# A transformer block on eight cores: pacing weight casts, keeping x on chip, contiguous attention tiles, and re-ordered weight loads

## The chip, the cores and the metric

The kernel runs on the 8 cores of one Trainium2 chip (two dies, cores 0 to 3 and 4 to 7). The batch has four sequences of 4096 tokens. Each core owns half a sequence (2048 tokens), reads the keys of the other half itself, and never talks to another core. The metric is the device time of the slowest core in microseconds (us). Fast executions of one kernel agree closely (eight of the kernel before, in the rounds of e9_all: 4768.13 to 4791.93 us, 0.5% apart). Some executions fall into a slower state, in which the cores of one die, or of both, show a lower TensorE clock (0.814 to 0.818 on one die in a run of the changed kernel, 5048.91 us; 0.895 to 0.903 on both in one of e9_all, 4639.74 us; against 0.976 to 0.986 in the fast runs of these two); those runs are marked slow and are not compared with fast ones.

Five engines matter: PE (TensorE, matmul), ACT (ScalarE, exponentials and casts), DVE (VectorE), POOL (GpSimd) and SP (SyncE, which here only issues transfers). The GpSimd queue also issues the transfers that convert float32 to bfloat16 on the way ("casts").

## The reference, cut to what matters

```python
D_MODEL, BATCH, SEQ = 2048, 4, 4096          # FFN_HIDDEN = 5632, head width 128
def _hybrid_layer(x, w_in, ...):
    qa, ka, va, qb, kb, vb, ga, gb = split(x @ w_in)
    # A: 8 query heads, 2 key/value heads, full attention over 4096 keys
    out_a = _gqa_blocks(rope(rms(qa)) * scale, rope(rms(ka)), va)          # (B, S, 1024)
    # B: 12 heads in 3 groups with dilation 1, 4, 16; 129 keys per query;
    #    the three groups are combined weighted by their softmax denominators
    out_b = _dilated_window_attention(qb * scale, kb, vb)                  # (B, S, 512)
    mixed = (sigmoid(ga + b0) * (out_a @ w_proj_a)
             + sigmoid(gb + b1) * (out_b @ w_proj_b)) @ w_out
    x = layer_norm(ALPHA * x + mixed)
    h = silu(x @ w_ffn_gate) * (x @ w_ffn_up)
    return layer_norm(ALPHA * x + h @ w_ffn_down)
```

## The kernel before

A small scheduler records every operation, derives the semaphores from which tiles it reads and writes, and emits each engine's instructions in program order. Each engine works through its own list in that order; the timelines below show it for VectorE, which stands idle 1.22 us ahead of a sum whose input is not ready. The stages follow one another:

1. QKV of A for the core's own tokens and keys of all 4096.
2. Attention A: 32 blocks (8 heads by 4 token blocks) of 16 steps. Between the steps, PE is fed "filler" matmuls: B's K, V and Q projections. Their results are copied out of PSUM by VectorE and stored to memory. In the same stage the GpSimd queue casts the later weights to bfloat16 in memory.
3. Attention B, with some of the gate projections as filler.
4. Merge, output projection with the first norm, feed-forward, and a tail.

Cuts are marked with three dots:

```python
# the casts of later weights: 1 MB written by each, issued in attention A's loop
for kc in range(0, 16, 2):
    pre.append((wo_s[kc:kc + 2], wo_d[kc:kc + 2], [("wo", kc), ("wo", kc + 1)]))
for j in range(22):
    pre.append((wfg_s[j], wfg_d[j], [("wg", j)]))
    pre.append((wfu_s[j], wfu_d[j], [("wu", j)]))
...
# filler: one 512-column result is copied to one of three small buffers and stored
def stage_out(bk, n, dst_list, key):
    g = SG[sg_n[0] % 3]
    sg_n[0] += 1
    s.copy("dve", g[:, 0:n], bk[:, 0:n])
    for dst, src in dst_list(g):
        s.dma("sp", dst, src, wk=[key])
...
# attention A, one step
s.actf(pt[:, :], sp_t[:, :], AF.Exp, scale=SCALE)
...
fil.run_to(min(1.0, (G + 1) / NPC))
...
precast_to(int((G + 1) * 88 / NPC))
```

```python
# attention B: a "quad" is four 128-query tiles. Tiles of dilation 4 and 16 are read with that stride.
for j in range(4):
    quads.append((hh, 0, [(0, 4 * j + a) for a in range(4)], j))
    quads.append((hh, 1, [(a, j) for a in range(4)], j))
...
    s.mm(st[...], BK[g][:, kk:kk + dil * 127 + 1:dil], BQ[g][:, q0:q0 + dil * 127 + 1:dil])
    s.stt(st3[...], st3[...], SCALE, bb[...], ALU.mult, ALU.add)          # bias, VectorE
    s.actf(pb[:, :], st[:, :], AF.Exp)                                    # ScalarE
    s.tt("dve", DS[t % 3][...], pb4[:, :, 0, :], pb4[:, :, 1, :], ALU.add)  # sum of key pairs
    ...  # two quads later: probabilities times V into num, sums into den;
    ...  # dilation 4 is accumulated in PSUM on top of dilation 1
    o = num[:, a * 128:(a + 1) * 128] if g != 1 else num[:, r:512:4]
    ...
    elif g == 1:
        s.tt("dve", ACD[:, cs], den, ACD[:, cs], ALU.add)
        s.tt("dve", ACN[:, cs], num, ACN[:, cs], ALU.add)
        s.actf(ACD[:, cs], ACD[:, cs], AF.Ln)
        s.actf(ACD[:, cs], ACD[:, cs], AF.Exp, scale=-1.0)
        s.tt("dve", OB[hh][:, cs], ACN[:, cs], ACD[:, cs], ALU.mult)
```

```python
# output projection: norm and cast of a token tile follow its matmuls
p6_ln(tt)        # statistics and centring on VectorE, scale and shift on GpSimd
p6_cast(tt)      # ScalarE: bfloat16 copy for the transposes
...
# feed-forward: ScalarE's SiLU after each column group
s.actf(sg[:, :], pg, AF.Silu)
```

The softmax here doesn't subtract the row's maximum and nothing guards it: scores larger than these inputs give would overflow.

## Time and profile before

The three runs that set the baseline gave 4788.51, 4779.18 and 4795.51 us. The profiled execution's slowest core is core 4, 4789.8 us long. The stages below are cut at events: the first exponential of attention A, the first of attention B, the first matmul of the merge, of the output projection and of the feed-forward, and the last matmul. Spans are medians over the eight cores, in us.

| stage | span before |
|---|---|
| QKV of A | 272.8 |
| attention A with B's projections | 1480.1 |
| attention B | 211.7 |
| merge | 608.4 |
| output projection | 288.3 |
| feed-forward | 1857.6 |
| tail | 51.7 |

The page of the kernel before: busy time per engine, then the span in 40 slices with PE's busy share, PE's granted clock and the DMA engines' busy share in tenths.

```profile
PE 4141.3 (86%) x19504; PEld 1906.2 (40%) x19504; DVE 1244.5 (26%) x1842; ACT 1005.3 (21%) x1221; POOL 485.4 (10%) x374
...
PE   7953867666998888989889979999999999999995
...
PEclk9976989888999989999999999999999999999997
DMA  8676376386345347331223556555545554554533
```

PE is the engine that bounds it, and its largest holes are in slices 3 to 15. The table by stretches of the kernel before, cut at core 4's stages (start and end, length, then busy us of PE, weight loads, DVE, ACT and POOL with counts, the mean granted PE clock, the DMA share and GB/s), for attention A, attention B, merge and feed-forward:

```profile
274.30:1765.60 1491.30, 1079.42 (x4826) 475.57 (x4827) 475.68 (x723) 560.31 (x577) 71.78 (x138) 0.87 0.55 83
1765.60:1983.50 217.90, 192.96 (x1189) 113.19 (x1188) 119.09 (x160) 94.94 (x118) 6.72 (x13) 0.93 0.68 168
1983.50:2589.60 606.10, 548.63 (x2433) 242.37 (x2432) 132.41 (x193) 89.95 (x131) 29.22 (x55) 0.95 0.23 44
...
2879.50:4738.10 1858.60, 1838.50 (x8480) 829.58 (x8480) 220.37 (x327) 142.93 (x217) 108.25 (x24) 0.99 0.51 170
```

Attention A lasts 1491 us for 1079 us of PE work; the feed-forward has no room. PE's waits before (waiting engine and line, what released it, us in total, times, the longest):

```profile
PE pbig L156 <- DVE SG_111 L192: 128.4, 16, 32.1
PE pbig L156 <- DVE SG_112 L192: 114.2, 15, 44.1
PE pbig L156 <- DVE SG_113 L192: 93.1, 18, 21.5
...
PE pbig L156 <- DMA WG_186<-wfg_s: 32.0, 1, 32.0
PE pbig L156 <- DMA WGT_160<-wgb: 23.6, 4, 8.3
```

336 us are waits for VectorE to copy a filler result into one of the three SG buffers. VectorE is not slow: one copy takes 0.68 us. It waits for the buffer, whose store has not landed (the largest of these waits; us in total, times, the longest):

```profile
DVE SG_111 L192 <- DMA vb_s<-SG_111: 89.3, 3, 35.9
```

At the same time the casts on the GpSimd queue take this long from issue to landing (count, KB, median us):

```profile
wfg_s<-wfg POOLq DMA_DIRECT2D x22, 1024.0 KB, 44.2
...
wo_s<-wo POOLq DMA_DIRECT2D x8, 1024.0 KB, 55.8
```

In attention B the strided tiles cost PE time. The score matmuls of dilation 16 and of dilation 4 before (duration in ns: shortest, median, longest):

```profile
L156 PE MATMUL pbig<-BQ_121,BK_124 x128: 398/422/428, 1762.0 to 1943.0; 128*128 128x128 bf16 x128
...
L156 PE MATMUL pbig<-BQ_123,BK_126 x128: 275/297/314, 1783.9 to 1973.2; 128*128 128x128 bf16 x128
```

The same tile of dilation 1 takes 219 ns. Last, a view that the prediction looked at too little: VectorE's timeline over one pair of quads (dilation 1 and 4) in attention B before. Columns: start us, duration us, engine, line, operation, output and inputs, and in brackets how long the engine sat idle just before and what ended it.

```profile
1920.58 0.43 DVE L176 TENSOR_TENSOR DS_136<-PB_133 128x512 bf16<-128x512 bf16 x1 [1.22 <-ACT PB_133 L170]
1920.93 0.68 DVE L176 TENSOR_TENSOR ACD_120<-pbig,ACD_120 128x512 f32<-128x512 f32 x1
1921.53 0.68 DVE L176 TENSOR_TENSOR ACN_119<-pbig,ACN_119 128x512 f32<-128x512 f32 x1
1923.23 0.69 DVE L176 TENSOR_TENSOR OB_117<-ACN_119,ACD_120 128x512 bf16<-128x512 f32 x1 [1.02 <-ACT ACD_120 L170]
1923.84 1.23 DVE L188 SCALAR_TENSOR_TENSOR pbig<-pbig,BB_130 128x1024 f32<-128x1024 f32 x1
1926.29 0.43 DVE L176 TENSOR_TENSOR DS_137<-PB_134 128x512 bf16<-128x512 bf16 x1 [1.22 <-ACT PB_134 L170]
1926.63 1.23 DVE L188 SCALAR_TENSOR_TENSOR pbig<-pbig,BB_131 128x1024 f32<-128x1024 f32 x1
1929.07 0.43 DVE L176 TENSOR_TENSOR DS_138<-PB_135 128x512 bf16<-128x512 bf16 x1 [1.22 <-ACT PB_135 L170]
```

A pair takes 1929.07 - 1920.58 = 8.5 us. VectorE adds a bias, then stands 1.22 us until ScalarE's exponential of that same quad is done, because the sum DS is next in its list. It stands another 1.02 us for ScalarE's logarithm and exponential, because the product OB is next. Three such pauses, 3.5 us, belong to every pair although VectorE is busy only 119 us of the stage's 218.

### The profile page before, as it was taken

How to read it: one execution, taken by the hardware profiler on the slowest of the kernel's cores; microseconds unless marked ns; L12 is line 12 of the kernel's file. 1: busy time of each engine (PE TensorE's matmuls, PEld its weight loads, DVE VectorE, ACT ScalarE, POOL GpSimd, SP SyncE). 2: the span in 40 equal slices, each digit the busy share in tenths (PEclk: the TensorE clock that was granted, in tenths of full speed). 3: DMA queues.
4: the chain of work that ended last, by engine and by line, in shares of the span. 5: the costliest groups of instructions: out<-in, count | busy, mean ns of one | idle time of the engine just before them, and what ended most of it. 6: DMA issues, size and time to landing. Idle time of an engine off the chain costs nothing.

```text
span 4789.8 us, 50993 instructions; the slowest of 8 cores (4749.5 to 4789.8 us)
## 1 busy us (share of the span) xinstructions
PE 4141.3 (86%) x19504; PEld 1906.2 (40%) x19504; DVE 1244.5 (26%) x1842; ACT 1005.3 (21%) x1221; POOL 485.4 (10%) x374
## 2 busy tenths in 40 slices
PE   7953867666998888989889979999999999999995
PEld 4521323223343334534334434444444444444442
DVE  3531323322343335421112541100110111011102
ACT  1221434333454434311110211000110011001100
POOL 3320000000000000000000560000100011001103
PEclk9976989888999989999999999999999999999997
DMA  8676376386345347331223556555545554554533
GB/s 133 135 112 85 55 97 85 53 113 92 74 91 86 55 109 183 96 76 25 37 36 111 167 171 226 166 160 163 191 167 167 172 185 166 164 172 173 183 123 110
DMA packets 194974, 594.35 MB, mean 124 GB/s; under 512 B 53808, under 2 KB 102768, under 8 KB 162672
## 3 DMA queue, kind: packets, MB, share of 16 engines
q1 hardware_dynamic: 167504, 444.21, 28.5%
q0 software_dynamic: 27232, 146.88, 21.8%
q8 instruction: 160, 2.62, 0.2%
q14 instruction: 78, 0.64, 0.0%
HBM read 668.03 MB, written 147.46 MB: 170 GB/s over the span
## 4 chain that ended last, share of the span: by engine, by line
PE 73%; DMA 12%; another core or an unknown queue 5%; DVE 3%; issue 2%; POOL 2%; ACT 2%; SPq 1%; POOLq 0%; DVEq 0%; ACTq 0%
PE pbig L156 72%; DMA kb_s<-SG_112 2%; DMA vb_s<-SG_113 2%; SPq L146 1%; DMA qb_s<-SG_113 1%; DMA kb_s<-SG_113 1%; DMA XF_73<-xT 1%; DMA WV_76<-wva 1%; DMA WGT_160<-wgb 1%; DMA WGT_162<-wgb 1%; POOL YY_177 L176 1%; PE pbig L154 1%; DMA kb_s<-SG_111 1%; DMA WR_101<-wvb 1%
## 5 line engine op out<-in xcount | busy, mean ns | idle before, releaser
L170 ACT ACTIVATE SGL_205<-pbig 128x512 f32<-128x512 f32 x88 | 52.6, 598 | 947.3 <-PE pbig L156 947.2
L156 PE MATMUL pbig<-WD_193,HT_192 128*128 128x512 bf16 x944 | 224.4, 384 | 10.0 <-DMA WD_193<-wfd_s 9.3
L156 PE MATMUL pbig<-WD_194,HT_192 128*128 128x512 bf16 x944 | 220.6, 381 | 4.6 <-DMA WD_194<-wfd_s 4.3
L156 PE MATMUL pbig<-WD_195,HT_192 128*128 128x512 bf16 x928 | 218.4, 383 | 5.5 <-DMA WD_195<-wfd_s 5.2
L176 DVE TENSOR_TENSOR HT_192<-SGL_206,pbig 128x512 bf16<-128x512 f32 x88 | 60.5, 688 | 536.2 <-PE pbig L156 536.2
L176 DVE TENSOR_TENSOR HT_192<-SGL_205,pbig 128x512 bf16<-128x512 f32 x88 | 60.6, 688 | 503.5 <-PE pbig L156 499.1
L170 ACT ACTIVATE PT_106<-pbig 128x1024 bf16<-128x1024 f32 x128 | 131.1, 1025 | 236.2 <-PE pbig L156 197.7
L170 ACT ACTIVATE PT_105<-pbig 128x1024 bf16<-128x1024 f32 x128 | 131.1, 1024 | 203.2 <-PE pbig L156 152.3
L170 ACT ACTIVATE PT_107<-pbig 128x1024 bf16<-128x1024 f32 x128 | 131.2, 1025 | 176.6 <-PE pbig L156 128.0
L188 DVE SCALAR_TENSOR_TENSOR YY_154_196<-XR_158_200,pbig 128x512 f32<-128x512 f32 x16 | 11.0, 688 | 585.7 <-PE pbig L156 585.7
L176 POOL TENSOR_TENSOR YY_154_196<-YY_154_196,LNP_162_204 128x2048 f32<-128x2048 f32 x8 | 36.9, 4608 | 1231.4 <-DVE YY_154_196 L183 1230.8
L170 ACT ACTIVATE SGL_206<-pbig 128x512 f32<-128x512 f32 x88 | 52.6, 597 | 510.3 <-PE pbig L156 510.3
L170 ACT ACTIVATE PT_108<-pbig 128x1024 bf16<-128x1024 f32 x128 | 130.6, 1020 | 98.4 <-PE pbig L156 77.7
L156 PEld LDWEIGHTS pbig<-WD_193,HT_192 128*128 128x128 bf16 x944 | 92.7, 99 | 125.9 <-issue 18.6
L156 PEld LDWEIGHTS pbig<-WD_194,HT_192 128*128 128x128 bf16 x944 | 92.3, 98 | 117.9 <-issue 8.7
L156 PE MATMUL pbig<-X1T_184,WG_186 128*128 128x512 bf16 x480 | 111.4, 386 | 32.0 <-DMA WG_186<-wfg_s 32.0
L156 PEld LDWEIGHTS pbig<-WD_195,HT_192 128*128 128x128 bf16 x928 | 91.1, 99 | 118.4 <-issue 11.9
L170 ACT ACT_TABLE_LOAD x29 | 37.2, 1283 | 352.8 <-DVE MV_52 L994 249.2
L156 PE MATMUL pbig<-X1T_184,WU_191 128*128 128x512 bf16 x480 | 108.5, 379 | 0.0
L156 PE MATMUL pbig<-X1T_184,WU_189 128*128 128x512 bf16 x480 | 108.5, 379 | 0.0
L156 PE MATMUL pbig<-X1T_185,WU_190 128*128 128x512 bf16 x480 | 108.5, 379 | 0.0
L156 PE MATMUL pbig<-X1T_185,WG_187 128*128 128x512 bf16 x480 | 108.5, 379 | 0.0
(766 smaller groups left out, 7284.8 us busy)
## 6 DMA issues: line engine op xcount, KB each, us to landing
WG_186<-wfg_s SPq DMA_DIRECT2D x30, 1024.0 KB
WU_189<-wfu_s SPq DMA_DIRECT2D x30, 1024.0 KB
WD_193<-wfd_s SPq DMA_DIRECT2D x59, 512.0 KB
WD_194<-wfd_s SPq DMA_DIRECT2D x59, 512.0 KB
WG_187<-wfg_s SPq DMA_DIRECT2D x29, 1024.0 KB
WU_190<-wfu_s SPq DMA_DIRECT2D x29, 1024.0 KB
WG_188<-wfg_s SPq DMA_DIRECT2D x29, 1024.0 KB
WU_191<-wfu_s SPq DMA_DIRECT2D x29, 1024.0 KB
```

The lines of the kernel that those rows point to most:

```text
L146: return self.add(q, lambda e: e.dma_start(out=out, in_=in_), ins, outs, rk, wk, dma=True)
L154: fn = lambda e: e.matmul(out, lhsT=lhsT, rhs=rhs, start=start, stop=stop, skip_group_check=True)
L156: fn = lambda e: e.matmul(out, lhsT=lhsT, rhs=rhs, start=start, stop=stop)
L170: return self.add("act", lambda e: e.activation(out=out, in_=in_, func=func, **kw), ins, [out])
L176: return self.add(eng, lambda e: e.tensor_tensor(out=out, in0=a, in1=b, op=op), [a, b], [out])
L188: return self.add("dve", lambda e: e.scalar_tensor_tensor(out=out, in0=a, scalar=sc, in1=b, op0=op0, op1=op1), ins, [out])
```

## The change

Its intent, part by part:

- **Casts:** half-size (0.5 MB written), each waiting for an exponential of attention A so that they come evenly; 32 of the down-projection's casts move to the merge.
- **x kept on chip:** two buffers of 16 KB per partition hold the far x; their last contents are what B's halo needs, so it is not loaded again. B's K and Q are staged per head in one buffer KS and stored once per head.
- **B's tiles:** K and Q are stored residue by residue, so every tile is contiguous. Dilation 4 is then no longer in token order with dilation 1, so it gets its own evacuation with strided adds.
- **Merge:** gate A of all four token blocks, then gate B, so each weight tile is done sooner. All of B's first loads are issued ahead.
- **Output projection and feed-forward:** weights prefetched; the transposes of the last tiles moved.
- **Tail:** the last half of the last down projection runs tile by tile from 22 resident weight tiles, so only the last tile's norm follows the last matmul.

The diff, cut to its core (cuts marked):

```diff
     for j in range(22):
-        pre.append((wfg_s[j], wfg_d[j], [("wg", j)]))
-        pre.append((wfu_s[j], wfu_d[j], [("wu", j)]))
+        for q in range(2):
+            c = slice(q * 2048, (q + 1) * 2048)
+            pre.append((wfg_s[j][:, c], wfg_d[j][:, c], [("wg", j, q)]))
+            pre.append((wfu_s[j][:, c], wfu_d[j][:, c], [("wu", j, q)]))
...
-            s.dma("pool", o, i, wk=k)
+            s.dma("pool", o, i, wk=k, after=after)
...
-        self.n_dma = {"sp": 16, "pool": 8}
+        self.n_dma = {"sp": 24, "pool": 16}
...
+    far = [(6, 0), (7, 1), (4, 0), (5, 1)]          # last two stay in XH for B's halo
+    for i, (tb, b) in enumerate(far):
+        pair_mms(WK, XH[b], tb, 1, k_dst(tb))
...
+                        if dil == 1:
+                            s.copy("dve", KS[:, tb * 512:tb * 512 + n], bk[:, 0:n])
+                        else:
+                            i0 = tb * 512 // dil
+                            s.copy("dve", KS[:, 0:tot].rearrange("p (r i) -> p r i", r=dil)[:, :, i0:i0 + n // dil],
+                                   bk[:, 0:n].rearrange("p (i r) -> p r i", r=dil))
+                        if tb == nt_list[-1][0]:
+                            s.dma("sp", dst[:, 0:tot], KS[:, 0:tot], wk=[key])
...
-            s.actf(pt[:, :], sp_t[:, :], AF.Exp, scale=SCALE)
+            ex = s.actf(pt[:, :], sp_t[:, :], AF.Exp, scale=SCALE)
+            precast_to(NPRE * (G + 1) // NPC, ex)
```

```diff
         for j in range(4):
+            quads.append((hh, 1, [(a, j) for a in range(4)], j))
             quads.append((hh, 0, [(0, 4 * j + a) for a in range(4)], j))
-            quads.append((hh, 1, [(a, j) for a in range(4)], j))
...
-                    s.mm(st[...], BK[g][:, kk:kk + dil * 127 + 1:dil], qap)
+                    s.mm(st[...], k_tile(g, r, k0), q_tile(g, r, n))
...
             elif g == 1:
+                def view(t_):
+                    return t_[:, cs].rearrange("p (i r) -> p r i", r=4)
+                s.tt("dve", view(ACN), num.rearrange("p (a c) -> p a c", c=128), view(ACN), ALU.add)
+                s.tt("dve", view(ACD), den.rearrange("p (a c) -> p a c", c=128), view(ACD), ALU.add)
+            else:
                 s.tt("dve", ACD[:, cs], den, ACD[:, cs], ALU.add)
                 s.tt("dve", ACN[:, cs], num, ACN[:, cs], ALU.add)
...
+    p6_ln(14)
+    p6_cast(14)
+    p6_ln(15)
+    p6_cast(15)
...
-    late_tr = [14, 15]
+    late_tr = [13, 14, 15]
...
+    WDF = [at("WDF", ...) for i in range(22)]       # resident weights of the last half
...
+    for tl in range(4):                             # last half, one token tile at a time
+        for fb in range(2):
+            for hp in range(22):
+                ... s.mm(b, HT[...], WDF[hp][...], hc == 0, hc == NHC - 1)
+            evac(tl, 1, fb, b)
```

## The prediction

> **What bounds it now.** TensorE: the page gives 86% busy, the other engines at most 26%. In fully busy stretches a 128x512 matmul issues every 215 to 217 ns (table by stretches: 465 per 100 us, clock 1.00), so only PE's holes can shrink. [...] here all eight hold 0.99 through the feed-forward[...]. By stage (span us, PE busy):
> - QKV of A: 0-275, 242
> - attention A with B's projections as filler: 275-1740, 1070
> - attention B: 1740-1985, 203
> - merge: 1985-2592, 550
> - output projection: 2592-2880, 237
> - feed-forward: 2880-4740, 1838
> - tail: 50, PE idle
>
> **Attention A holds the gain.** PE's waits: 336 us for VectorE's copies into the three SG buffers, which themselves wait for SG's stores to land (chain: 25 to 50 us each); 37 us for the first WR. The pool queue's timeline shows why: after reloading XH it fires weight casts as fast as slots free (1 MB written per 9.4 us, DMA share 1.02 at 300-400 us); small stores queue behind. Undisturbed (1246-1348, 1415-1513 us) a block of 16 steps takes 32.7 us, so 32 take 1050, not 1467. The change keeps x on chip, paces half-size casts by the exponentials, moves 32 to the merge, and stores K/Q once per head. Left over: waits for the single KS buffer, VectorE's strided copies: I allow 60. Stage about 1110: **-355**.
>
> **Attention B.** Matmuls on dilation-16 tiles take 422 ns against 225 for dilation 1 (busy 33.3 against 10.3 us per 128)[...]. Contiguous tiles save about 23+7 us; start and reload waits 16.3+11.8 largely vanish. VectorE then binds with PE (about 3.1 and 3.3 us per quad). 245 to about 180: **-65**.
>
> **Merge.** 57 us of waits for WGT (11, up to 8 us), because three buffers are released too late; finishing one gate over all four token blocks gives the load ~20 us. New: the first WGT now overlays DS, so about 9 us of wait at the stage's start. 607 to about 545: **-62**.
>
> **Output projection.** The WO wait (5) and 32 us WG wait at its end go, as WO streams in while X frees up and WG/X1T are prefetched: 288 to about 250: **-38**.
>
> **Feed-forward.** Same matmuls; WD waits (19 us) mostly stay, three transposes move in; in the last block WD and resident WDF together want ~1 MB per 3.4 us, near the 320 GB/s implied by 205 GB/s at share 0.64: up to 10 us lost. **0**.
>
> **Tail.** Only the last token tile's norm follows the last matmul: 50 to about 11: **-39**. First block's finer loads: **-6**.
>
> **Sum:** -565 would give 4225; I allow 15 for interactions: **4240 us**, 80% range 4160 to 4345. Faster by over 2%: 0.97; within 2%: 0.02; slower: 0.01.
>
> **Right if:** the waits on SG fall from 336 to under 50 us; attention A lasts 1070 to 1150; BQ/BK matmuls of all dilations take ~225 ns; WGT waits shrink to one; PE busy about 95%; under 15 us after the last matmul.
> **Wrong if:** VectorE waiting for KS stalls the exponentials at each of 24 heads (+50 to 100); evenly paced casts still delay stores; pool-queue waits for exponentials delay WR or WGT loads; DMA saturates in the last down half; denser work lowers the granted clock.

## The result, and the profile after

The changed kernel's results are correct. Its fast runs took 4347.99 and 4352.03 us. Executions in which one die ran at a lower clock are left out of the means. The ratio of fast runs is 0.9086, with a 95% interval of 0.9048 to 0.9124. It is the mean time of one kernel's fast runs over the mean time of the other's fast runs of the same rounds. The change is faster by 9.1%. That is 110 us short of the predicted 4240, and the fast runs lie 3 to 7 us above the predicted range.

Profiled cores: 4326.0 to 4346.5 us after, against 4749.5 to 4789.8 before. The span of each stage (medians over eight cores, us) beside the prediction's figure:

| stage | before | after | predicted after | after minus predicted |
|---|---|---|---|---|
| QKV of A | 272.8 | 273.4 | 269 | +4 |
| attention A | 1480.1 | 1138.4 | 1110 | +28 |
| attention B | 211.7 | 238.2 | 180 | +58 |
| merge | 608.4 | 527.4 | 545 | -18 |
| output projection | 288.3 | 260.9 | 250 | +11 |
| feed-forward | 1857.6 | 1882.2 | 1860 | +22 |
| tail | 51.7 | 18.2 | 11 | +7 |

The last column adds up to +112. One caution about the row of attention B: the prediction cut the stages where PE changed over, which put B's first load wait (16 us) and the first steps into B, so it started from 245 where this table has 212. In the changed kernel that wait is 1.6 us, so the two ways of cutting lie close together after the change; A and B together (1376 against 1290 predicted) miss by 86 whichever is used.

The page of the kernel after, the lines that answer to those above:

```profile
PE 4069.0 (94%) x19504; PEld 1874.6 (43%) x19504; DVE 1286.9 (30%) x1890; ACT 1009.5 (23%) x1229; POOL 496.6 (11%) x434
...
PE   7989999989989678999989799999999999999998
...
PEclk9999999999999898999999899999999999999999
```

The table by stretches after, cut at core 1's stages: attention A, attention B, merge and feed-forward.

```profile
274.50:1417.00 1142.50, 1052.45 (x4815) 469.86 (x4813) 475.21 (x723) 559.88 (x578) 76.50 (x143) 0.97 0.49 86
1417.00:1658.00 241.00, 166.18 (x1193) 90.67 (x1194) 151.30 (x195) 96.17 (x120) 10.25 (x20) 0.88 0.71 164
1658.00:2186.80 528.80, 527.43 (x2433) 238.46 (x2434) 132.03 (x192) 88.08 (x129) 44.40 (x85) 1.00 0.43 86
...
2446.10:4328.30 1882.20, 1837.56 (x8497) 828.92 (x8495) 258.85 (x380) 154.27 (x233) 142.12 (x40) 0.99 0.49 170
```

Read attention B across the two tables: PE's busy time fell from 193 to 166 us, as intended, while the stage grew from 218 to 241. DVE's busy time grew from 119 to 151. In the feed-forward PE's work is the same and the stage is 24 us longer. In the merge the same 2433 matmuls took 548.6 us before and 527.4 after, at a mean clock of 0.95 and 1.00.

PE's waits after:

```profile
PE pbig L158 <- DVE KS_112 L194: 59.9, 32, 7.5
PE pbig L156 <- DVE ACN_130 L178: 43.6, 24, 2.4
PE pbig L158 <- ACT SGL_205 L172: 19.4, 1, 19.4
...
PE pbig L158 <- ACT XBF_179 L175: 12.2, 1, 12.2
...
PE pbig L158 <- DMA WGT_164<-wga: 7.9, 1, 7.9
```

The 336 us for SG are down to 24.6 (four buffers), with 59.9 for KS beside them. Two lines are new: 43.6 us for ACN (attention B) and a single wait of 19.4 us for SGL (the feed-forward's start). The casts and the dilation-16 matmuls after:

```profile
wfg_s<-wfg POOLq DMA_DIRECT2D x44, 512.0 KB, 6.5
```

```profile
L158 PE MATMUL pbig<-BQ_115,BK_118 x128: 217/219/314, 1437.7 to 1636.6; 128*128 128x128 bf16 x128
```

The casts land in 6.5 us rather than 44.2, and the tiles of dilation 16 cost 219 ns rather than 422. VectorE's timeline over one pair of quads (now dilation 4 and 1) after:

```profile
1504.67 0.43 DVE L178 TENSOR_TENSOR DS_135<-PB_132 128x512 bf16<-128x512 bf16 x1 [1.22 <-ACT PB_132 L172]
1505.01 1.05 DVE L178 TENSOR_TENSOR ACN_130<-pbig,ACN_130 128x512 f32<-128x512 f32 x1
1505.97 1.06 DVE L178 TENSOR_TENSOR ACD_131<-pbig,ACD_131 128x512 f32<-128x512 f32 x1
1506.94 1.22 DVE L190 SCALAR_TENSOR_TENSOR pbig<-pbig,BB_124 128x1024 f32<-128x1024 f32 x1
1509.38 0.42 DVE L178 TENSOR_TENSOR DS_136<-PB_133 128x512 bf16<-128x512 bf16 x1 [1.22 <-ACT PB_133 L172]
...
1512.02 0.69 DVE L178 TENSOR_TENSOR OB_127<-ACN_130,ACD_131 128x512 bf16<-128x512 f32 x1 [1.02 <-ACT ACD_131 L172]
1512.63 1.23 DVE L190 SCALAR_TENSOR_TENSOR pbig<-pbig,BB_125 128x1024 f32<-128x1024 f32 x1
1515.08 0.42 DVE L178 TENSOR_TENSOR DS_137<-PB_134 128x512 bf16<-128x512 bf16 x1 [1.22 <-ACT PB_134 L172]
```

The three pauses are all still there, and two adds of 1.05 us are new: the pair takes 1515.08 - 1504.67 = 10.4 us instead of 8.5. There are 16 such pairs, so 16 x 1.9 = 31 us, against 26.5 that the stage grew.

ScalarE's timeline after, at the start of the feed-forward:

```profile
2462.24 1.90 ACT L175 CAST XBF_181<-YY_177 128x2048 bf16<-128x2048 f32 x1 [11.46 <-POOL YY_177 L178]
...
2475.42 1.90 ACT L175 CAST XBF_179<-YY_178 128x2048 bf16<-128x2048 f32 x1 [11.08 <-POOL YY_178 L178]
...
2478.63 0.60 ACT L172 ACTIVATE SGL_205<-pbig 128x512 f32<-128x512 f32 x1
```

The first SiLU (SGL) runs only after the casts of the last two token tiles, which stand 11 us each for GpSimd's norm products. PE, out of PSUM banks, stands with it (19.4 us).

### The profile page after: what moved, and what is told of

Its sections match the earlier page's. It is cut to its first block, busy times and chain, and to the rows that moved or that the text cites. A ratio compares the mean times of both kernels' runs of the same rounds, so it can differ in the third digit from the quotient of the medians.

```text
span 4346.5 us, 50922 instructions; the slowest of 8 cores (4326.0 to 4346.5 us)
## 1 busy us (share of the span) xinstructions
PE 4069.0 (94%) x19504; PEld 1874.6 (43%) x19504; DVE 1286.9 (30%) x1890; ACT 1009.5 (23%) x1229; POOL 496.6 (11%) x434
## 4 chain that ended last, share of the span: by engine, by line
PE 82%; DMA 7%; DVE 4%; ACT 3%; issue 2%; POOL 1%; SPq 0%; DVEq 0%; ACTq 0%; POOLq 0%
PE pbig L158 82%; DMA kb_s<-KS_112 1%; DVE pbig L190 1%; DMA WD_193<-wfd_s 1%; DMA WD_194<-wfd_s 1%; DMA X_59<-xT 1%; DMA WD_195<-wfd_s 1%; DMA qb_s<-KS_112 1%; DVE KS_112 L194 1%; DVE ACD_131 L178 1%; DMA WV_77<-wva 0%; ACT PT_105 L172 0%; POOL YY_177 L178 0%; POOL YY_178 L178 0%; ACT ACD_131 L172 0%
## 5 line engine op out<-in xcount | busy, mean ns | idle before, releaser
L158 PE MATMUL pbig<-WD_193,HT_192 128*128 128x512 bf16 x832 | 196.6, 383 | 8.9 <-DMA WD_193<-wfd_s 8.3
L158 PE MATMUL pbig<-WD_194,HT_192 128*128 128x512 bf16 x816 | 190.8, 381 | 8.1 <-DMA WD_194<-wfd_s 7.8
L158 PE MATMUL pbig<-WD_195,HT_192 128*128 128x512 bf16 x816 | 190.3, 379 | 8.1 <-DMA WD_195<-wfd_s 7.8
L178 POOL TENSOR_TENSOR YY_154_196<-YY_154_196,LNP_162_204 128x2048 f32<-128x2048 f32 (+1 forms) x10 | 32.4, 3240 | 1152.7 <-DVE YY_154_196 L185 998.3
L158 PEld LDWEIGHTS pbig<-WD_193,HT_192 128*128 128x128 bf16 x832 | 81.3, 99 | 111.4 <-issue 17.1
L158 PEld LDWEIGHTS pbig<-WD_194,HT_192 128*128 128x128 bf16 x816 | 79.7, 98 | 107.4 <-issue 13.9
L158 PEld LDWEIGHTS pbig<-WD_195,HT_192 128*128 128x128 bf16 x816 | 79.2, 98 | 106.2 <-issue 11.8
L158 PE MATMUL pbig<-X1T_184,WG_187 128*128 128x512 bf16 x448 | 104.2, 387 | 19.4 <-ACT SGL_205 L172 19.4
L158 PE MATMUL pbig<-X1T_184,WU_191 128*128 128x512 bf16 x480 | 108.5, 379 | 0.0
L158 PE MATMUL pbig<-X1T_184,WG_186 128*128 128x512 bf16 x480 | 108.5, 379 | 0.0
L158 PE MATMUL pbig<-X1T_184,WU_189 128*128 128x512 bf16 x480 | 108.5, 379 | 0.0
L158 PE MATMUL pbig<-X1T_185,WG_186 128*128 128x512 bf16 x480 | 108.5, 379 | 0.0
L158 PE MATMUL pbig<-X1T_185,WU_189 128*128 128x512 bf16 x480 | 108.5, 379 | 0.0
```

The costliest lines, as they stand in the source:

```text
L158: fn = lambda e: e.matmul(out, lhsT=lhsT, rhs=rhs, start=start, stop=stop)
L178: return self.add(eng, lambda e: e.tensor_tensor(out=out, in0=a, in1=b, op=op), [a, b], [out])
```

## The experiments

Twelve kernels ran. All gave correct results. All but e9_all were without timed rounds. Their stage spans, medians over the eight cores in us:

| kernel | attention A | attention B | merge | output proj. | feed-forward | tail | whole |
|---|---|---|---|---|---|---|---|
| before | 1480.1 | 211.7 | 608.4 | 288.3 | 1857.6 | 51.7 | 4772.2 |
| after | 1138.4 | 238.2 | 527.4 | 260.9 | 1882.2 | 18.2 | 4339.1 |
| e1_merge | 1134.5 | **222.4** | 527.1 | 260.6 | 1885.5 | 18.2 | 4332.6 |
| e2_ds_late | 1134.9 | **212.5** | 527.5 | 258.4 | 1883.3 | 18.2 | 4307.6 |
| e7_p3_order | 1142.2 | **189.4** | 527.3 | 257.2 | 1881.7 | 18.2 | 4282.6 |
| e12_before_order | 1474.2 | **202.1** | 605.8 | 289.7 | 1860.4 | 51.7 | 4758.4 |
| e3_cast_late | 1138.2 | 238.8 | 527.5 | 257.5 | **1858.6** | 18.2 | 4312.9 |
| e4_ks_ring | **1126.0** | 238.6 | 527.3 | 258.4 | 1883.4 | 18.2 | 4324.9 |
| e5_unpaced | **1169.5** | 257.5 | 527.1 | 257.3 | 1888.7 | 18.2 | 4392.9 |
| e10_full_unpaced | **1229.8** | 234.4 | 527.3 | 257.9 | 1885.0 | 16.5 | 4420.1 |
| e6_before_paced | **1169.0** | 213.3 | 607.8 | 285.5 | 1860.2 | 51.7 | 4458.6 |
| e11_before_half | **1271.5** | 214.1 | 605.0 | 289.2 | 1861.4 | 54.0 | 4565.5 |
| e8_nocast | **1122.2** | 722.0 | 527.6 | 258.0 | 1882.5 | 18.2 | 4801.4 |
| e9_all | 1129.0 | 197.4 | 527.5 | 256.7 | 1858.2 | 18.3 | 4256.6 |

Stages that an experiment leaves alone repeat closely (the merge within 0.5 us in all variants of the changed kernel), on four different chips, so stages are compared. Attention A repeats less closely: in the five kernels that share the changed kernel's version of it (after, e1, e2, e3, e7) it lasts 1134.5 to 1142.2 us, so a difference of 8 us there says nothing. The kernels were derived from the changed kernel, except e6, e11 and e12, which were derived from the kernel before.

### Attention B: VectorE's list, or throughput, or the loads?

The theory: attention B is a chain through VectorE's in-order list; the two strided adds lengthen it and the pauses for ScalarE sit in it. The rivals: the engines' throughput, or the loads of the next head.

**e1_merge** takes the extra evacuation out again: dilation 4 is accumulated in PSUM on dilation 1, with contiguous tiles kept.

```diff
-            quads.append((hh, 1, [(a, j) for a in range(4)], j))
             quads.append((hh, 0, [(0, 4 * j + a) for a in range(4)], j))
+            quads.append((hh, 1, [(a, j) for a in range(4)], j))
...
-                o = num[:, a * 128:(a + 1) * 128]
+                o = num[:, a * 128:(a + 1) * 128] if g != 1 else num[:, r:512:4]
...            # start and stop flags set so that g == 1 adds to g == 0; one evacuation for both
```

> The changed kernel with one part undone: dilation 4 again accumulates onto dilation 1 in PSUM, so one evacuation serves both (q, k stay residue-major). Theory V (attention B is a chain through VectorE's in-order queue: bias add, wait for the exponential, sum, evacuation; the change added two strided adds of 1.05 us per pair to it): a dilation-1 plus dilation-4 pair goes from 10.4 us to about 8.4 us, the stage from 239 to about 205 us, fast time about 4315. Rival P (TensorE's own work or its waits for transfers bound the stage): the stage grows a little, since the strided PSUM writes cost TensorE some 1.1 us per pair.

Measured: attention B 222.4 us, 16 less than the changed kernel. PE's wait for ACN fell from 43.6 to 18.4 us, but 15.1 us of waits for the next head's BK appeared (1.6 before). The extra evacuation is real and costs about what the timeline said, of which the reload gives half back. With everything else on contiguous tiles, the stage is still no shorter than in the kernel before (211.7): the faster tiles alone gained nothing. (In this run cores 0 and 1 had a longer QKV stage, 309 and 317 us; the other six were ordinary in that stage. It happened once more, to the same two cores in e5_unpaced. Cores 2 and 3 of e1 had a longer feed-forward, 1909 and 1913 us. The medians of attention B are not touched by it.)

**e2_ds_late** keeps the extra evacuation and only moves the sum DS of a quad behind the bias step of the next quad, where its exponential has long been done.

```diff
+            ds_sum(t - 1)                    # ahead: DS of the quad before
             pb = PB[t % 3]
             ex = s.actf(pb[:, :], st[:, :], AF.Exp)
-            s.tt("dve", DS[t % 3][...], pb4[:, :, 0, :], pb4[:, :, 1, :], ALU.add)
```

> The changed kernel with only the order of VectorE's queue in attention B changed: the sum over key halves of quad t-1 is issued behind the bias add of quad t, instead of that of quad t, which sits 1.22 us waiting for the exponential. No instruction is added or removed. Theory V: the pair falls from 10.4 to about 8.5 us, a dilation-16 quad from 3.8 to about 3.3, the stage from 239 to about 200 us, fast time about 4310. Rival T (throughput of the strided evacuations or of TensorE bounds it, not the order): stage within 10 us of 239.

Measured: 212.5 us, 25.7 less (200 was expected), without removing one instruction. A pair takes 7.8 us instead of 10.4. By the pair alone that would be 16 x 2.6 = 42 us; 19.4 us of waits for BK took the rest, since now the loads come late. That refutes throughput as the limit of the changed kernel.

**e7_p3_order** adds two more moves: the product OB is issued one quad late, and the next head's Q, K and bias are loaded as soon as the last quad that reads them has issued its bias step.

```diff
-                s.tt("dve", OB[hh][:, cs], ACN[:, cs], ACD[:, cs], ALU.mult)
+                ob_pend.append(ob)           # issued behind the next bias step
...
+            if g != 2 and j == 3 and hh < 3:
+                load_bq(hh + 1, g)           # right behind the last bias step of this group
             ds_sum(t - 1)
+            while ob_pend:
+                ob_pend.pop(0)()
```

> The changed kernel with the order of attention B alone changed, further than in e2: sums one quad late, the last product of a pair one quad late (it waited 1.02 us for ScalarE's logarithm and exponential), and the next head's q, k and bias loads issued right behind the last use of the old ones instead of two quads later (BK waits were 19 us in e2). If the in-order queues and the late reloads are the rest of the cost: a pair falls from 7.8 to about 6.9 us, BK waits under 6 us, the stage from 212 to about 180 us, which is the figure that was forecast from throughput. If TensorE or the transfers bind now: over 200.

Measured: 189.4 us, 49 less than the changed kernel, with the same arithmetic. VectorE's timeline in this kernel (core 1), part of a pair:

```profile
1506.86 1.24 DVE L190 SCALAR_TENSOR_TENSOR pbig<-pbig,BB 128x1024 f32<-128x1024 f32 x1
1507.99 0.43 DVE L178 TENSOR_TENSOR DS<-PB 128x512 bf16<-128x512 bf16 x1
1508.33 0.69 DVE L178 TENSOR_TENSOR OB<-ACN,ACD 128x512 bf16<-128x512 f32 x1
1508.93 1.07 DVE L178 TENSOR_TENSOR ACN<-pbig,ACN 128x512 f32<-128x512 f32 x1
...
1513.57 1.21 DVE L190 SCALAR_TENSOR_TENSOR pbig<-pbig,BB 128x1024 f32<-128x1024 f32 x1
```

No line has a bracket: VectorE is never idle in the pair, which takes 6.7 us. This is the VectorE-bound state that the prediction assumed ("about 3.1 and 3.3 us per quad", so 6.6 us at most for two). What remains above 180 are waits that the pair does not show: 10.3 us for the first gate weight (WR), 9.1 for ZS and 7.8 for BV.

**e12_before_order** gives the kernel before only the two moves of DS and OB, with its strided tiles.

```diff
+            ds_sum(t - 1)                    # DS of the quad before, then OB of the quad before
+            while ob_pend:
+                ob_pend.pop(0)()
             pb = PB[t % 3]
             s.actf(pb[:, :], st[:, :], AF.Exp)
-            s.tt("dve", DS[t % 3][...], pb4[:, :, 0, :], pb4[:, :, 1, :], ALU.add)
```

> The kernel before with only VectorE's order in attention B changed (sums one quad late, the pair's last product one quad late); q and k stay strided. It asks whether the residue-major tiles were worth anything there. If VectorE's chain limited this stage before too and TensorE's strided tiles were hidden under it: a pair falls from 8.5 us to TensorE's own 7.2, a dilation-16 quad stays near 4.4, the stage goes from 212 to 190 to 200, and the residue-major tiles with the same order (e7, 189) are worth only some 10 us more. If the order did not matter before: 212 within 6.

Measured: 202.1 us, 9.6 less than before. The pair takes 1838.67 - 1831.44 = 7.2 us (core 4), and now VectorE waits for PE:

```profile
1837.47 0.69 DVE L176 TENSOR_TENSOR ACD<-pbig,ACD 128x512 f32<-128x512 f32 x1 [1.89 <-PE pbig L154]
```

With both kernels in a good order the contiguous tiles are worth 202.1 - 189.4 = 13 us. e7 also loads its next head earlier, so the tiles alone may be worth less. In the wrong order they were hidden, and what they brought with them (the strided adds) was not.

### Attention A: which part of the change freed the stores?

The theory put first was pacing; the rival was everything else (half-size casts, x kept on chip, one store per head, fewer casts). Seven kernels make a ladder:

| kernel | x kept, stores per head | MB per gate or up cast | MB cast in the stage (at most in flight) | paced | attention A | median landing of the gate's casts |
|---|---|---|---|---|---|---|
| before | no | 1 | 70 (8 casts) | no | 1480 | 44.2 |
| e11_before_half | no | 0.5 | 70 (16 casts) | no | 1272 | 35.2 |
| e10_full_unpaced | yes | 0.5 | 70 (8 casts) | no | 1230 | 22.0 |
| e5_unpaced | yes | 0.5 | 52 (16 casts) | no | 1169 | 20.0 |
| e6_before_paced | no | 1 | 70 (8 casts) | yes | 1169 | 9.0 |
| after | yes | 0.5 | 52 (16 casts) | yes | 1138 | 6.5 |
| e8_nocast | yes | 0.5 | 0 | no casts | 1122 | not in the stage |

**e5_unpaced** takes pacing alone out of the changed kernel.

```diff
-            s.dma("pool", o, i, wk=k, after=after)
+            s.dma("pool", o, i, wk=k)
```

> The changed kernel with the pacing alone undone: casts no longer wait for an exponential, the pool queue issues them as slots come free (16 now). If pacing is what freed attention A: waits for SG and KS come back to some 250 us or more and the stage goes from 1134 to 1350 or more, time 4550 or more. If keeping x on chip and storing K and Q once per head did it: the stage stays under 1200.

Measured: 1169.5 us, only 31 more than with pacing. PE's wait for KS rose from 59.9 to 87.7 us. Attention B also lost 19 us, to a longer wait for BK (27.1 us).

**e6_before_paced** puts pacing alone into the kernel before.

```diff
-            s.dma("pool", o, i, wk=k)
+            s.dma("pool", o, i, wk=k, after=after)
...
-        precast_to(int((G + 1) * 88 / NPC))
+        precast_to(int((G + 1) * 88 / NPC), ex)     # ex: this step's exponential
```

> The kernel before with the pacing alone added: each 1 MB cast waits for the exponential of its step; sizes, counts and stores as before. If pacing alone suffices: waits for SG fall from 336 to under 80 us, attention A from 1467 to 1180 or less, time about 4500. If the stores per tile and the reloaded x matter as much: it stays over 1250.

Measured: 1169.0 us, 311 less than before, and the whole kernel 4480.87 us against some 4790. The three SG buffers, the small stores and the reloaded x, all left as they were, cost PE 69.6 us of waits instead of 336. So pacing alone gets nearly all of the gain, and so does the rest without pacing. The parts do not add up: each removes the same waits.

**e8_nocast** issues no casts in attention A at all, to see the floor.

```diff
-            precast_to(NPRE * (G + 1) // NPC, ex)
```

> Wrong result on purpose: the changed kernel without any weight cast during attention A (all 148 casts then come late or not at all in time, so later stages read uncast scratch; only attention A is read). If the remaining waits there (KS 60, SG 25 us) come from casts crowding the stores: both fall under 25 us in sum and the stage comes near 1060. If a store simply takes longer than the slack to land: KS waits stay over 40 us, the stage stays over 1100.

Measured: 1122.2 us in attention A. The casts were meant to be left out, but the later stages' loop caught up on them: all came out in attention B, which took 722 us, and the result stayed correct. For attention A the answer is clear: all casts together now cost 16 us. The floor of 1050 that the prediction took from the undisturbed stretches is not reached without any cast. From one block's end to the next, most blocks of 16 steps take 33.4 to 36.9 us here; the 32.7 us of the two calm stretches were among the best blocks, not a typical one (1122 / 32 = 35.1). PE still waits 48.3 us for KS and 24.6 for SG. These waits are what separates the stage from 1050: on the slowest core PE's own work is 1049 of 1127 us. So 1050 was right as the work, and wrong as the length of a stage without casts.

**e4_ks_ring** gives B's query heads a second KS buffer, in the place of one of five weight buffers.

```diff
+    KSR = [KS, at("KSB", 178, [128, T], BF16)]
...
+        KS = KSR[(li - 24) % 2] if li >= 24 else KSR[0]
```

> The changed kernel with a second staging buffer for the 12 Q heads in attention A (it takes the place of the fifth weight buffer once K and V are done); the 12 K heads keep the single one. Theory K (TensorE waits for VectorE, which waits for the one KS buffer's store to land): waits on KS fall from 60 to about 35 us, those of the Q half vanish, the stage gets 15 to 25 us shorter, fast time about 4330. Rival D (VectorE is late for its own work at block ends, KS is only the name on it): waits keep their sum under the new buffer's name and the stage keeps its 1134 us within 8.

Measured: 1126.0 us, 12 less than the changed kernel and 8.5 less than the shortest of the four others with the same stage, so the gain is small and not sharply measured; 15 to 25 were expected. The waits for KS fell to 42.5 us, with 9.5 for the second buffer: 8 us less in sum. VectorE no longer waits for a store of a query head (20.8 us in the changed kernel), but still 27.8 us for those of the key heads, which keep the single buffer. Of PE's 42.5 us, 12 come behind such a wait; behind the rest VectorE had not waited, so there PE waits for the copy itself, which has to empty the bank. That the copy is strided is not the reason: a copy into KS takes 0.68 us, as one into SG does.

**e11_before_half** and **e10_full_unpaced** look at what "the rest" is. e11 gives the kernel before half-size casts alone, with 16 outstanding instead of 8, so the same bytes of them outstanding. The casts for the output projection and the down projection stay as they were.

```diff
-        pre.append((wfg_s[j], wfg_d[j], [("wg", j)]))
-        pre.append((wfu_s[j], wfu_d[j], [("wu", j)]))
+        for q in range(2):
+            c = slice(q * 2048, (q + 1) * 2048)
+            pre.append((wfg_s[j][:, c], wfg_d[j][:, c], [("wg", j, q)]))
+            pre.append((wfu_s[j][:, c], wfu_d[j][:, c], [("wu", j, q)]))
...
-        self.n_dma = {"sp": 16, "pool": 8}
+        self.n_dma = {"sp": 16, "pool": 16}
```

> The kernel before, still unpaced, with each gate and up weight cast split into two half-size casts (rows half as long, 16 slots so that the bytes under way stay the same). If long cast rows[...] made the stores slow: attention A from 1480 to 1330 or less. If it is the backlog of unpaced casts in whatever pieces: still over 1400.

Measured: 1271.5 us, 209 less than before, for the same bytes in the same stage. PE's waits for SG fell from 336 to 172 us:

```profile
PE pbig L156 <- DVE SG L192: 172.4, 42, 34.3
```

e10 takes pacing out of the changed kernel and puts the full volume of casts and 8 slots back.

```diff
-            precast_to(NPRE * (G + 1) // NPC, ex)
+            precast_to((NPRE + 36) * (G + 1) // NPC, ex)     # and no wait for ex
...
-        self.n_dma = {"sp": 24, "pool": 16}
+        self.n_dma = {"sp": 24, "pool": 8}
```

> e5 (changed kernel, casts not paced) with as many casted bytes in attention A as before (140 instead of 104 half-size casts) and 8 slots on the pool queue as before. If volume or slots made the difference between e5 (1169 us) and before (1480): attention A over 1300. If the changed stores and cast sizes did: under 1220.

Measured: 1229.8 us.

What follows: of the unpaced gain, the largest piece comes with splitting the gate and up casts (1480 to 1272). The step from e11 to e10 (1272 to 1230) joins keeping x on chip, storing per head, half the bytes in flight and the splitting of the output projection's casts. Casting 52 MB rather than 70 in the stage is worth another 60 (1230 to 1169, although with twice as much in flight).

A reason for the first piece may be the length of the packets in which the casts travel: small stores may be held up more beside long packets. This is the author's guess; no run shows a store waiting for a packet. The packet records of the kept traces agree with it:

- In attention A of the kernel before (core 4), 2256 packets of the GpSimd queue carried 32 KB each and took 4.5 us (median). Packets of 4 KB took 0.32 us. The split casts travel in packets of 4 KB.
- In e11, 960 packets of 32 KB are left, those of the casts that were not split. On its core 0, the three blocks of attention A in which over 100 of them ran hold 23, 45 and 48 us of PE's waits for VectorE. None of the other 29 blocks holds over 3.1 us, though in several of them some 1000 packets of 4 KB passed in 35 us, as many bytes per us as in the block of 48 us (290 packets of 32 KB in 87 us).
- The down-projection casts are of 0.5 MB in every kernel and still travel in packets of 32 KB; one of the three blocks is theirs, and so are the two largest waits of e10 (27 and 16 us, core 7). So it is the packet, not the size of the cast, that goes with the waits.
- The first two of the three blocks are those of the output projection's casts: 68 us of waits, against 10 in the same blocks of e10, where these casts are split. That can account for the 41 us between e11 and e10, though the other parts of that step act there too.

Pacing helps with long packets too (in e6 PE's waits for SG are 69.6 us instead of 336). No run varies packet length with everything else fixed, so this reading rests on the comparison of blocks within a run.

### The start of the feed-forward

**e3_cast_late** issues the two casts of the last token tiles ahead of the third and the fourth round of the feed-forward (each round is two column groups) instead of ahead of the first.

```diff
     p6_ln(14)
-    p6_cast(14)
     p6_ln(15)
-    p6_cast(15)
...
+            if tb == 0 and j in (2, 3):
+                p6_cast(12 + j)
```

> The changed kernel with the last two casts of the output projection (tiles 14 and 15) issued on ScalarE only behind the first two column groups of the feed-forward. Theory Q (ScalarE's in-order queue holds the first SiLU behind casts that wait for the last LayerNorm): TensorE's 19.4 us wait for SGL goes, output projection start to feed-forward end gets 16 to 19 us shorter, fast time about 4332. Rival L (weights or x1T landing late, or VectorE held by the same LayerNorm, is right behind it): another wait of 10 us or more takes its place and under 8 us are gained.

Measured: feed-forward 1858.6 us, 23.6 less, as long as in the kernel before (1857.6). PE's wait for SGL is gone from its list. ScalarE's timeline in this kernel (core 1):

```profile
2448.68 1.09 ACT L172 ACTIVATE SGL<-pbig 128x512 f32<-128x512 f32 x2
...
2461.81 1.89 ACT L175 CAST XBF<-YY 128x2048 bf16<-128x2048 f32 x1
```

The SiLUs now come first, and a cast that comes later finds its input ready: no bracket.

### All together

**e9_all** joins e3, e4 and e7, and four smaller moves: the filler of attention B starts three quads later, the merge's first weight goes into another of its three buffers, its first gate runs for all token blocks ahead of the first product, and the first transpose of the output projection comes later.

```diff
-        fil.run_to(min(1.0, (t + 0.5) / NQ))
+        fil.run_to(min(1.0, max(0.0, (t - 2.5) / (NQ - 3))))
...
-            s.dma("pool", WGT[k % 3][:, :, :], (wga_d, wgb_d)[ab][f])
+            s.dma("pool", WGT[(k + 1) % 3][:, :, :], (wga_d, wgb_d)[ab][f])
...            # in the merge's first pass, gate A of all token blocks ahead of their projections
-            if fb == 1:
+            if fb == (3 if tt == 2 else 1):
                 p6_tr(tt - 2)
```

> All that helped together: attention B as in e7, late casts as in e3, second staging buffer for Q heads as in e4, first transposes of the output projection half a tile later (a 12 us wait), no filler in attention B's first three quads (10 us wait for its weights), the merge's first weight in a buffer that is free earlier and its first gate before its first product (6 to 8 us). Sum of the stages: qkv 271, attention A 1127, attention B 172, merge 521, output projection 250, feed-forward 1859, tail 18: about 4218 us on the median core, fast time about 4232, ratio to the kernel before about 0.884, to the changed kernel about 0.973. If the gains merely uncover other waits (weights of the feed-forward, x1T): over 4270.

Measured: fast runs of 4266.22, 4282.12 and 4269.68 us; the ratio to the kernel before is 0.894, interval 0.8913 to 0.8966. The interval lies wholly below that of the changed kernel (0.9048 to 0.9124). So this version beats both kernels, the changed one by about 1.6% (0.894 / 0.9086), though the two were not timed in the same rounds. Of the sum of single gains (49 + 24 + 12 = 85) the whole shows 82. The forecast of 4232 was missed by 34 to 50 us, and the fast runs lie on both sides of the 4270 that stood for "other waits are uncovered": attention B (197 for 172) and the output projection (257 for 250) fell short. The four smaller moves did little. The merge's first wait (7.7 us) is still there, so that buffer was not its cause. Attention B is 197.4 rather than 189.4, with 9.9 us of waits for BK, so starting the filler later, if anything, hurt there. The wait for XBF in the output projection fell from 12.2 to 5.6.

## Why the prediction was right or wrong, point by point

The direction (faster by over 2%, chance 0.97) was right, and so was "Attention A holds the gain". The size was off by 110 us.

- **Attention B, "VectorE then binds with PE (about 3.1 and 3.3 us per quad)" (wrong, the largest miss: 180 predicted, 238 measured).** This step took sums of busy time for a pace. The pair of quads took 10.4 us, not 6.6, because VectorE worked its list in order and stood three times per pair for ScalarE, as the brackets of 1.22, 1.22 and 1.02 us show. "Contiguous tiles save about 23+7 us" was right for PE (193 to 166 us busy) and worth nothing to the stage, because PE did not set its pace. VectorE's list did, and the two adds of 1.05 us made it longer. e7 reached 189 by order alone (VectorE's, and that of the loads), with a pair of 6.7 us, so the pace named was the right one for a kernel that has the right order.
- **Attention A, -355 (nearly right: 1110 predicted, 1138 measured).** The cause (stores stuck behind casts) was right: e6 and e11 show it from the side of the kernel before (PE's waits for SG 69.6 and 172 us instead of 336). The mis-sized term is what is left over, "I allow 60": on core 1 PE's waits in the stage come to 87 us. KS has 59.9 of them, as allowed, but SG's 24.6 come on top, and e8 shows that these stay without any cast. The base, "32 take 1050", was right as PE's own work (1052 us busy in the changed kernel, 1049 in e8), with some luck: in the kernel before, the eight blocks between 1236 and 1504 us take 33.5 us each, waits included, not 32.7. The prediction also did not see that the parts are redundant, nor that the clock would rise: for nearly the same matmuls PE was busy 1079 us before and 1052 after, at a mean clock of 0.87 and 0.97.
- **Feed-forward "0" (wrong: +22).** That the "32 us WG wait at its end" goes was right. Behind it lay another: the two casts in ScalarE's list ahead of the first SiLU (19.4 us for PE), and e3 removed it (-23.6). It was there before in part, covered by the wait for WG: in the kernel before the last cast ended 20.5 us after the last matmul of the output projection, while PE got its first WG only after 31.3 us. The rest the change made itself, by interleaving the matmuls of the last two token tiles, so that both norms come after them: the last cast now ends 31.1 us after that matmul (medians over the cores). WD waits stayed as predicted (18.8 us before, 23.9 after).
- **Output projection, 250 (measured 261).** Both waits named went. The wait of 12.2 us for XBF, in the list of waits before as 12.5, stayed, and one of 4.9 us for XTS is new.
- **Merge, 545 (measured 527, better).** WGT waits did shrink to one, of 7.9 us ("about 9 us"). The prediction took PE's busy time of 550 us as about the floor. It was not one: on core 4 before, the clock's record falls to 0.5 for 3.4 or 6.8 us at each of eleven holes of 3.8 to 8.3 us, and is back 2.7 to 5.9 us after the hole's end; after, no hole inside the stage is over 1.4 us. The same 2433 matmuls took 527.4 us at a mean clock of 1.00, 548.6 at 0.95.
- **Tail, 11 (measured 18.2).** The mechanism was right. The mis-sized term is the last tile's norm: VectorE's steps over 640 columns took 0.88 us alone but 1.43 to 1.71 while GpSimd ran its own products, and the span ends 9.7 us after VectorE's last step, with the stores of that tile on their way. Why VectorE's steps were longer beside GpSimd's, no run shows.
- **The clock.** The prediction read 0.99 on all eight cores through the feed-forward of the kernel before, and named a lower clock under "wrong if". It did not come in the fast runs: a mean of 0.976 to 0.981 on all eight cores, over the whole span.
- **The list "right if":** waits on SG under 50 (24.6, yes, though KS took a part of them over); attention A 1070 to 1150 (1138, yes); score tiles at about 225 ns (219, yes); one WGT wait (yes); PE busy about 95% (94%, yes); under 15 us after the last matmul (18.2, no). Five of six came true and the total was still 110 us off, because none of them looked at the pace of the stage that failed. Of the list "wrong if", the stall at KS was named with +50 to 100; PE's waits for KS were 59.9 us, within the allowance of 60, and a second buffer for half of the heads took 8 of them away (e4).

Open: how the 41 us between e11 and e10 divide between the split casts of the output projection, keeping x on chip, storing per head and the smaller number of bytes in flight; what packet length does alone; and how much of e7's lead over e12 is the tiles and how much the earlier loads.

## What to carry to other kernels

In a stage where several engines hand work around, take its pace from one period of the timeline, brackets included, not from busy time: here an instruction that waited for another engine held up everything behind it in its list (VectorE stood 1.22, 1.22 and 1.02 us in each pair of quads), and moving it behind the next independent instruction gained more (25.7 us for one sum, 49 with one product and earlier loads) than the shorter matmuls of contiguous tiles (at most 13). When a long wait is taken away, look for what stood behind it in each engine's list, because a wait that ended earlier was free until then. When several parts of a change remove the same wait, test each alone on the kernel before: pacing alone gave 311 us of the 342 that attention A gained.

## What was measured of the hardware here

- In the fast runs of the changed kernel all eight cores held a mean TensorE clock of 0.976 to 0.981, and 1.00 in the full merge stage. In a slow run (5048.91 us) the cores of one die showed 0.814 to 0.818 and the other die 0.98. So here the low clock came in some runs, in this one on one die, and not in every all-core run.
- Score tiles read at a stride of 4 elements (8 bytes) took 297 ns against 219 contiguous; at 16 elements 422. PE's ends are modelled in the trace, but the starts agree: within a burst a tile starts 56 ns after the one before it when contiguous, 118 at a stride of 4, 240 at 16.
- In attention A of the kernel before, a packet of 32 KB took 4.5 us and one of 4 KB 0.32; a gate, up or output-projection cast landed in 44 to 56 us unpaced and in about 6 us paced and halved, and PE's waits behind the stores were 336 and 85 us (SG and KS).
- A VectorE add of 128x512 whose float32 tile is strided by 16 bytes took 1.05 us, against 0.69 contiguous.
- VectorE's list in its order, not its busy time, set the pace of attention B: three pauses of 1.22, 1.22 and 1.02 us in a pair of quads of 10.4 us.
